# A down projection by seven products: additions to the residual given a later place in the schedule, and one weight difference formed later

## Chip, cores and metric

The kernel runs on one core of one Trainium2 chip. The metric is the device time of one execution in microseconds, lower being better. The kernel before took 1417.21 us (the median of three runs, 1415.67 to 1417.69). Data lies in HBM; SyncE issues the transfers (DMAs) of weights into SBUF, TensorE multiplies into banks of PSUM, VectorE and ScalarE work on SBUF and PSUM. Each engine takes its instructions in the order in which they were put into its queue.

## The reference, cut to what matters

The program is a decoder trunk of two layers over 512 tokens and 1024 features: a gated DeltaNet mixer with a gated MLP behind it, then sliding-window attention with a gated MLP. The change lies in the last product of the MLPs, the down projection (`@ w_down` below), whose result is added to the residual stream `h`.

```python
SEQ = 512; D_MODEL = 1024; D_FF = 2816
def rmsnorm(x, w):
    xf = x.astype(jnp.float32)
    y = xf * lax.rsqrt(jnp.mean(xf * xf, axis=-1, keepdims=True) + EPS)
    return (y * w.astype(jnp.float32)).astype(x.dtype)
...
# every layer: a mixer, then
#   u, g = up projection of rmsnorm(h); a causal convolution of width 3; act(.) * (.)
#   h = h + (that) @ w_down          # 512 x 2816 times 2816 x 1024
# and, behind the last layer, a final rmsnorm
```

## The kernel before, in words

**Layout.** Features lie on the 128 partitions and tokens along the free axis: `h[m]`, for m = 0 to 7, is a tile of 128 features by 512 tokens (the first pair shows in the trace as `h`, pairs behind it as `h` or `pz`). The 2816 inner features of the MLP are 22 tiles of 128.

**A product in three.** Each f32 operand is split into a high part (`whi`, `xh`: a cast by ScalarE, L132, L155, L172) and the rest (`wlo`, `xl`: a subtraction by VectorE, L133, L156, L173). Each product of two tiles is three matmuls: high by high, high by low, low by high. In the up and other projections these are L162 to L164, 512 tokens wide; in the down projection L1052 to L1054, 256 wide.

**The MLP.** `ffn` takes the inner features in two halves, of 12 tiles (six pairs) and of 10 (five pairs). For each half it computes the up projections and forms from them the operands of the seven products (`forms`: VectorE at L1001 to L1007). Then it runs the down projection of this half for the eight output tiles, as four pairs `m2`. So there are four such stretches in the program, two in each layer. The last pair of the last one is computed directly (`last_mm`, L957 to L970) and goes straight into the final norm (`final`, from L1102).

**Seven products (L1039 to L1099).** A block product of two by two blocks (two of inner features and two of output features for the weights, and two halves of the tokens for the inputs) takes seven products of blocks in place of eight. Their inputs are sums and differences of blocks. Weights are combined in place by VectorE: A21 += A22 (L1063), A11 = A21 - A11 (L1071), A12 -= A11 (L1072) and A22 -= A11 (L1080), in a `stage` tile which holds three (or two) pairs of inner tiles; `u` = 0 and 1 are the two `stage` tiles of one pair of output tiles. `cast` splits half 0 of such a tile (blocks A11 and A21) or half 1 (A12 and A22) when it is called; `cast_to(w4, ...)` splits A22 for the seventh product (L155, L156). The products add up in four banks of PSUM: `a` in a bank of tag d (3 buffers), `b` in g (2), `d` in s (2), and `c` in p (1), or in d for odd pairs; the seventh, `e`, is in g, or in p for odd pairs.

**Additions.** `add` (L1056 and L1057) adds a bank to quarters of the residual, on VectorE. With u = 1 four of them follow their products at once: bank a to h11, b to h11, d to h22, c to h21, each 128x256. At the end come bank a once more to three quarters (L1094, 128x768), bank d to h12 (L1095) and bank e to two quarters (L1098, 128x512). A bank is free for the next pair when its last addition has read it.

**What sets the order.** The code is written as generators whose steps are called in a fixed turn: the pairs m2 = 0 and 1 of a stretch in the turn 0, 1, 0, 0, 1, 1, then three steps of 2 and three of 3. From this program order a scheduler builds, before the program is compiled, the order of each engine's queue. An instruction has a priority from its place in the program; `tc.high_priority(n)` moves those inside it ahead, and a negative n puts them back. Buffers (`stage` has 2 and a third, `st`; `whi` and `wlo` have 3 each) are assigned at the same time. The next weights are loaded by SyncE (L1034) into a `stage` buffer once its last reader is done.

Of the kernel before, what the change touches and what calls it, by code (L numbers as in the profile page):

```python
# [12 lines left out]
ALU = mybir.AluOpType  # L13
# [4 lines left out]
P = 128  # L18
# [23 lines left out]
def kernel(  # L42
# [27 lines left out]
    V, S, G, PE, SP = nc.vector, nc.scalar, nc.gpsimd, nc.tensor, nc.sync  # L70
# [42 lines left out]
    def bank(tag):  # L113
        return psum.tile([P, T], F32, tag=tag, bufs=BANKS[tag], name=nm(tag))
# [13 lines left out]
    def cast(st, kt, half, m=P):  # L128
        hi = wpool.tile([P, 8, P], F32R, tag="whi", bufs=3, name=nm("whi"))
        lo = wpool.tile([P, 8, P], F32R, tag="wlo", bufs=3, name=nm("wlo"))  # L130
        src = st[:, :kt, half * P : half * P + m]
        S.copy(hi[:, :kt, :m], src)  # L132
        V.tensor_tensor(lo[:, :kt, :m], src, hi[:, :kt, :m].bitcast(F32), op=ALU.subtract)  # L133
        return hi, lo
# [14 lines left out]
    def weights():  # L149
        return [wpool.tile([P, 8, P], F32R, tag=t, bufs=3, name=nm(t)) for t in ("whi", "wlo")]  # L150

    def cast_to(w, at, src):
        n = src.shape[1]
        hi, lo = [t[:, at : at + n, :] for t in w]
        S.copy(hi, src)  # L155
        V.tensor_tensor(lo, src, hi.bitcast(F32), op=ALU.subtract)  # L156
# [106 lines left out]
    for k in range(KD):  # L263
        ps = bank("g") if k % 2 else bank("s")
# [502 lines left out]
    for i, line in enumerate(ORDER):  # L767
        for word in line.split():
            a, n = word[0], [int(d) for d in word[1:]]
# [41 lines left out]
    def wide(role):  # L811
        return pair(nxt("wide", YROLE), F32R)
# [6 lines left out]
    for h2 in range(HV // 2):  # L819
        a, b = wide("G"), wide("L")  # L820
# [26 lines left out]
    for m2 in range(KD // 2):  # L847
        sts = [load_stage(a_w_out[0], 1024 * u, 8, 256 * m2) for u in range(2)]
        for j in range(2):
            m = 2 * m2 + j  # L850
            ps = bank("d")
# [184 lines left out]

    def seven_products(sts, srcs, parts, sevens, hp, odd):  # L1039
        h11, h12, h21, h22 = [hp[:, i, HALF[u]] for i in range(2) for u in range(2)]  # L1040
        n = len(sevens)

        def blocks(u):
            e, o = slice(0, 2 * len(parts[u]), 2), slice(1, 2 * len(parts[u]), 2)
            return sts[u][:, e, 0:P], sts[u][:, o, 0:P], sts[u][:, e, P : 2 * P], sts[u][:, o, P : 2 * P]

        def product(ps, w, at, form, u, first=True, step=2):
            for i, k in enumerate(parts[u]):
                hi, lo = sevens[k][form]
                wk = at + step * i  # L1050
                kw = dict(skip_group_check=not first)
                PE.matmul(ps, w[0][:, wk, :], hi, start=first and k == 0, stop=False, **kw)  # L1052
                PE.matmul(ps, w[0][:, wk, :], lo, start=False, stop=False, **kw)  # L1053
                PE.matmul(ps, w[1][:, wk, :], hi, start=False, stop=k == n - 1, **kw)  # L1054

        def add(dst, ps):  # L1056
            V.tensor_tensor(dst, dst, ps, op=ALU.add)  # L1057

        a, b, d, c = [bank(t)[:, 0:256] for t in ("d", "g", "s", "d" if odd else "p")]
        for u in range(2):  # L1060
            A11, A12, A21, A22 = blocks(u)
            nk, end = len(parts[u]), u == 1
            V.tensor_tensor(A21, A21, A22, op=ALU.add)  # L1063
            w = cast(sts[u], 2 * nk, 0)
            product(a, w, 0, "B11", u)
            if end:
                add(h11, a)
            product(b, w, 1, "B21", u)
            if end:
                add(h11, b)  # L1070
            V.tensor_tensor(A11, A21, A11, op=ALU.subtract)  # L1071
            V.tensor_tensor(A12, A12, A11, op=ALU.subtract)  # L1072
            w = cast(sts[u], 2 * nk, 1)
            product(d, w, 0, "T1", u)
            if end:
                add(h22, d)
            product(c, w, 1, "T4", u)
            if end:
                add(h21, c)
            V.tensor_tensor(A22, A22, A11, op=ALU.subtract)  # L1080
            yield
        e = bank("p" if odd else "g")[:, 0:256]
        w4 = weights()
        for u in range(2):
            w = cast(sts[u], 2 * len(parts[u]), 0)
            product(a, w, 0, "T2", u, first=False)
            product(d, w, 1, "B22", u, first=False)
            cast_to(w4, 4 * u, blocks(u)[3])

        add(hp.rearrange("p u (v t) -> p (u v) t", v=2)[:, 1:4, :], a.unsqueeze(1).to_broadcast([P, 3, 256]))  # L1090
        add(h12, d)
        for u in range(2):
            product(e, w4, 4 * u, "T3", u, step=1)
        add(hp[:, 1, :].rearrange("p (u t) -> p u t", u=2), e.unsqueeze(1).to_broadcast([P, 2, 256]))  # L1094
        yield  # L1095


# [346 lines left out]
```

## Time and profile before

| what | value |
|---|---|
| three runs | 1417.21, 1415.67, 1417.69 us; median 1417.21 |
| profiled execution | span 1412.6 us; its own time is not printed beside it, the median lies 4.6 us above the span |
| traffic | 151.80 MB, 107 GB/s in the mean; queue q1 takes 33.2% of 16 DMA engines |
| L162, L163, L164 on TensorE | 1128 of each, 444.2, 444.0 and 441.9 us busy (overlapping) |
| L132 casts of `stage` on ScalarE | 234, 227.4 us, mean 976 ns |
| L133 corrections of `stage` on VectorE | 234, 263.4 us, mean 1128 ns |
| L133 corrections of `st` on VectorE | 30, 26.8 us, mean 899 ns |
| loads `stage` from w_down on SyncE's queue | 16 of 768 KB, 4.3 us from issue to landing |
| loads `st` from w_down | 8 of 768 KB, 5.3 us |

How to read it: the span is the time from the first to the last instruction of one profiled execution. An engine's busy share is a mean over stages with different limits, so what a change of one stage is worth is read from the waits in that stage. PE is the matmuls of TensorE, PEld its loads of the stationary operand, DVE is VectorE, ACT ScalarE, SP SyncE. A row of the timeline gives start, duration, engine, line, operation and tiles, and in brackets the idle time before it and what ended that.

### The profile page before, as it was taken

The page shows a single profiled execution, that of the slowest core. Times are in us where ns is not written, and L with a number is a line of the kernel's source. Part 1 is how long each engine was busy: PE and PEld are TensorE (multiplying, and loading weights), DVE is VectorE, ACT ScalarE, POOL GpSimd, SP SyncE. Part 2 cuts the span into 40 slices and gives each one's busy share as a digit, 9 for nine tenths or more (in the row PEclk, how much of TensorE's full clock was granted, in tenths as well). Part 3 has the DMA queues.
Part 4 walks back from the last instruction along what each step waited for, and adds up shares of the span by engine and source line. Part 5 has one row for each costly group of instructions (what it writes and reads, how often), then busy time and mean ns, then how long its engine had stood idle before and what let it go on. Part 6 is the DMA issues. An engine that isn't in the chain of part 4 may idle for free.

```text
span 1412.6 us, 21751 instructions
## 1 busy us (share of the span) xinstructions
PE 1384.7 (98%) x8370; PEld 1167.1 (83%) x8370; DVE 1108.1 (78%) x2070; ACT 748.1 (53%) x1470; POOL 15.6 (1%) x37
## 2 busy tenths in 40 slices
PE   7999999999999999999999999999999999999998
PEld 5787888878877888888988889777788888988897
DVE  4996896978856438879878889788668888878996
ACT  7764566656658225444344446567544444444543
POOL 1000000000100000000000000000000000000000
PEclk9999999999999999999999999999999999999999
DMA  5333254172465323221443223322132231432222
GB/s 161 92 103 115 79 175 126 61 231 84 140 225 159 119 90 112 90 90 46 135 150 119 75 79 109 109 71 76 61 112 90 90 101 49 146 106 82 92 75 75
DMA packets 162299, 151.80 MB, mean 107 GB/s; under 512 B 24148, under 2 KB 150677, under 8 KB 162197
## 3 DMA queue, kind: packets, MB, share of 16 engines
q1 hardware_dynamic: 159938, 150.22, 33.2%
q8 instruction: 66, 1.08, 0.3%
q10 hardware_dynamic: 2259, 0.20, 0.1%
q14 instruction: 36, 0.29, 0.1%
HBM read 133.60 MB, written 15.75 MB: 106 GB/s over the span
## 4 chain that ended last, share of the span: by engine, by line
PE 87%; DVE 6%; DMA 2%; ACT 2%; issue 1%; SPq 0%; DVEq 0%; ACTq 0%
PE d L162 20%; PE d L163 20%; PE d L164 20%; PE g L198 2%; DVE wlo L133 2%; PE d L1054 1%; PE d L1207 1%; PE d L1211 1%; PE d L1209 1%; PE d L1052 1%; PE d L1053 1%; PE s L1054 1%; PE s L1052 1%; PE s L1053 1%; PE s L659 1%
## 5 line engine op out<-in xcount | busy, mean ns | idle before, releaser
L162 PE MATMUL d<-xh,whi 128*128 128x512 f32 x1128 | 444.2, 394 | 0.2
L163 PE MATMUL d<-xl,whi 128*128 128x512 f32 x1128 | 444.0, 394 | 0.0
L164 PE MATMUL d<-xh,wlo 128*128 128x512 f32 x1128 | 441.9, 393 | 0.3 <-DVE wlo L156 0.3
L132 ACT CAST whi<-stage 128x1024 fp32r<-128x1024 f32 (+2 forms) x234 | 227.4, 976 | 247.7 <-PE d L163 165.1
L133 DVE TENSOR_TENSOR wlo<-stage,whi 128x1024 fp32r<-128x1024 f32 (+2 forms) x234 | 263.4, 1128 | 70.4 <-ACT whi L132 69.6
L162 PEld LDWEIGHTS d<-xh,whi 128*128 128x128 f32 x1128 | 211.7, 188 | 44.9 <-ACT xh L172 0.5
L164 PEld LDWEIGHTS d<-xh,wlo 128*128 128x128 f32 x1128 | 211.6, 188 | 44.6 <-DVE wlo L156 0.7
L163 PEld LDWEIGHTS d<-xl,whi 128*128 128x128 f32 x1128 | 211.7, 188 | 43.2 <-issue 0.5
L280 DVE SCALAR_TENSOR_TENSOR acc<-d,cwc,acc 128x511 f32<-128x511 f32 (+2 forms) x96 | 70.7, 739 | 8.7 <-ACT acc L277 7.9
L913 DVE TENSOR_TENSOR sz<-d,p6s 128x512 f32<-128x512 f32 x59 | 40.6, 688 | 42.9 <-PE d L164 40.7
L935 ACT ACTIVATE dt<-dt 128x512 f32<-128x512 f32 x44 | 27.8, 631 | 78.3 <-DVE dt L918 78.3
L918 DVE SCALAR_TENSOR_TENSOR dt<-sz,fcw,dt 128x511 f32<-128x511 f32 (+1 forms) x60 | 44.8, 747 | 1.8 <-ACT dt L916 0.9
L918 DVE SCALAR_TENSOR_TENSOR va<-sz,fcw,va 128x511 f32<-128x511 f32 (+1 forms) x58 | 43.3, 747 | 0.9
L561 DVE TENSOR_TENSOR sT<-sT,p6s 64x31 f32<-64x31 f32 (+15 forms) x124 | 40.9, 330 | 2.0
L555 DVE TENSOR_TENSOR p6s<-sN,sT 64x31 f32<-64x31 f32 (+15 forms) x124 | 40.7, 328 | 1.9
L1276 ACT ACTIVATE dt<-dt,sm 128x256 f32<-128x256 f32 (+1 forms) x64 | 30.1, 471 | 21.5 <-DVE sm L1259 21.5
L132 ACT CAST whi<-st 128x768 fp32r<-128x768 f32 (+1 forms) x30 | 23.7, 792 | 30.5 <-PE g L1053 9.0
L913 DVE TENSOR_TENSOR zl<-d,p6s 128x512 f32<-128x512 f32 x29 | 20.0, 688 | 17.8 <-PE d L164 17.8
L682 ACT ACTIVATE rq<-o 128x128 f32<-128x128 f32 x64 | 19.0, 301 | 25.4 <-DVE o L677 22.3
L937 DVE TENSOR_TENSOR va<-dt,va 128x512 f32<-128x512 f32 x44 | 30.4, 690 | 1.2
L133 DVE TENSOR_TENSOR wlo<-st,whi 128x768 fp32r<-128x768 f32 (+1 forms) x30 | 26.8, 899 | 2.2 <-ACT whi L132 2.2
L916 ACT ACTIVATE dt<-sz,normc,fcw 128x512 f32<-128x512 f32 x30 | 24.5, 815 | 6.5 <-DVE sz L913 6.0
(770 smaller groups left out, 2876.2 us busy)
## 6 DMA issues: line engine op xcount, KB each, us to landing
stage<-in_ffn_w_up_dram SPq DMA_DIRECT2D x44, 1024.0 KB, 4.8
stage<-in_a_w_in_dram SPq DMA_DIRECT2D x23, 1024.0 KB, 5.8
stage<-in_ffn_w_down_dram SPq DMA_DIRECT2D x16, 768.0 KB, 4.3
stage<-in_a_w_out_dram SPq DMA_DIRECT2D x8, 1024.0 KB, 5.0
st<-in_ffn_w_down_dram SPq DMA_DIRECT2D x8, 768.0 KB, 5.3
zd<-sz SPq DMA_DIRECT2D x16, 256.0 KB, 2.6
od<-o SPq DMA_DIRECT2D x16, 256.0 KB
stage<-in_b_w_q_dram SPq DMA_DIRECT2D x4, 1024.0 KB, 5.0
```

The source lines that it names most:

```text
L132: S.copy(hi[:, :kt, :m], src)
L133: V.tensor_tensor(lo[:, :kt, :m], src, hi[:, :kt, :m].bitcast(F32), op=ALU.subtract)
L162: PE.matmul(ps, hi[:, k, :m], xh[k], start=first and k == 0, stop=False)
L163: PE.matmul(ps, hi[:, k, :m], xl[k][:], start=False, stop=False)
L164: done.append(PE.matmul(ps, lo[:, k, :m], xh[k], start=False, stop=last and k == kt - 1))
L280: V.scalar_tensor_tensor(acc[:, d:], ps[:, : T - d], col, acc[:, d:], op0=ALU.mult, op1=ALU.add)
L555: V.tensor_tensor(tv, N[:, s, s + 1 : 32].unsqueeze(2).to_broadcast([64, n, m]), Tm[:, s : s + 1, 0:m].to_broadcast([64, n, m]), op=ALU.mult,)
L561: V.tensor_tensor(Tm[:, s + 1 : 32, 0:m], Tm[:, s + 1 : 32, 0:m], tv, op=ALU.subtract)
L913: V.tensor_tensor(u[:], ps[:], rs[:], op=ALU.mult)
L918: V.scalar_tensor_tensor(acc[:, d:], u[:, : T - d], tap(2 - d, t), acc[:, d:], op0=ALU.mult, op1=ALU.add)
L937: V.tensor_tensor(b[:], a[:], b[:], op=ALU.mult)
L1276: S.activation(ej, ej, AF.Exp, bias=ngm[:, i : i + 1], scale=-1.0, accum_out=den[:, i : i + 1])
```

## The change

All of it lies in `seven_products`. First, each addition to the residual is issued inside `tc.high_priority(-later)`, with `later` = 60 for the four that follow the products of u = 1, and END = 100 for the three at the end. Second, A22 -= A11 of both `u` is formed in the last step of the generator, just ahead of the `cast_to` that reads it, in place of the step of products T1 and T4.

```diff
+    END = 100
+
     def seven_products(sts, srcs, parts, sevens, hp, odd):
...
-        def add(dst, ps):
-            V.tensor_tensor(dst, dst, ps, op=ALU.add)
+        def add(dst, ps, later=60):
+            with tc.high_priority(-later):
+                V.tensor_tensor(dst, dst, ps, op=ALU.add)
...
             if end:
                 add(h21, c)
-            V.tensor_tensor(A22, A22, A11, op=ALU.subtract)
             yield
...
             product(a, w, 0, "T2", u, first=False)
             product(d, w, 1, "B22", u, first=False)
-            cast_to(w4, 4 * u, blocks(u)[3])
-
-        add(hp.rearrange("p u (v t) -> p (u v) t", v=2)[:, 1:4, :], a.unsqueeze(1).to_broadcast([P, 3, 256]))
-        add(h12, d)
+            A11, A12, A21, A22 = blocks(u)
+            V.tensor_tensor(A22, A22, A11, op=ALU.subtract)
+            cast_to(w4, 4 * u, A22)
+
+        add(hp.rearrange("p u (v t) -> p (u v) t", v=2)[:, 1:4, :], a.unsqueeze(1).to_broadcast([P, 3, 256]), END)
+        add(h12, d, END)
...
-        add(hp[:, 1, :].rearrange("p (u t) -> p u t", u=2), e.unsqueeze(1).to_broadcast([P, 2, 256]))
+        add(hp[:, 1, :].rearrange("p (u t) -> p u t", u=2), e.unsqueeze(1).to_broadcast([P, 2, 256]), END)
```

The numbers of instructions on every engine stay as they were (1967 rows on VectorE, 6929 on TensorE and 1030 on ScalarE), and SyncE's and GpSimd's queues keep their order. In the changed file the matmuls are L1054 to L1056, the addition is L1060, and the subtractions are L1066, L1074, L1075 and L1091. The scheduler gives other orders on VectorE, TensorE and ScalarE at three kinds of places.

**VectorE, first stretch of the first layer**, where pairs m2 = 0 and 1 overlap (`st_995`, `stage_6181` and `stage_6179` are weight tiles, `h_4550` is the residual; d, g, s and p are banks). Before:

```order
L1080 TENSOR_TENSOR st_995_6183<-st_995_6183 128x3x128
L133 TENSOR_TENSOR wlo_6293<-stage_6181,whi_6292 128x768
L133 TENSOR_TENSOR wlo_6319<-stage_6181,whi_6318 128x768
L1071 TENSOR_TENSOR stage_6181<-stage_6181 128x3x128
L1057 TENSOR_TENSOR h_4550<-h_4550,d_6187 128x256
L1072 TENSOR_TENSOR stage_6181<-stage_6181 128x3x128
L1057 TENSOR_TENSOR h_4550<-h_4550,g_6188 128x256
L1080 TENSOR_TENSOR stage_6181<-stage_6181 128x3x128
L1057 TENSOR_TENSOR h_4550<-h_4550,s_6189 128x256
L133 TENSOR_TENSOR wlo_6347<-stage_6179,whi_6346 128x768
L1057 TENSOR_TENSOR h_4550<-h_4550,p_6190 128x256
L156 TENSOR_TENSOR wlo_6345<-stage_6179,whi_6344 128x384
```

At the same place in the changed kernel:

```order
L133 TENSOR_TENSOR wlo_6291<-stage_6181,whi_6290 128x768
L133 TENSOR_TENSOR wlo_6317<-stage_6181,whi_6316 128x768
L1074 TENSOR_TENSOR stage_6181<-stage_6181 128x3x128
L133 TENSOR_TENSOR wlo_6344<-stage_6179,whi_6343 128x768
L1075 TENSOR_TENSOR stage_6181<-stage_6181 128x3x128
L156 TENSOR_TENSOR wlo_6342<-stage_6179,whi_6341 128x384
L1060 TENSOR_TENSOR h_4550<-h_4550,d_6187 128x256
L1091 TENSOR_TENSOR stage_6181<-stage_6181 128x3x128
L1060 TENSOR_TENSOR h_4550<-h_4550,g_6188 128x256
L1060 TENSOR_TENSOR h_4550<-h_4550,s_6189 128x256
```

The subtraction on `st` now stands behind these rows, and the correction and the split of `stage_6179` (L133 and L156) stand ahead of the four additions and not among and behind them.

**VectorE, end of the first layer** (behind the last products of the second stretch; `xl` are the low parts of the next norm's input, `f` and `gr` weights of the shared K/V projection, L866 sums squares). Before:

```order
L173 SCALAR_TENSOR_TENSOR xl_8389<-h_4550,normc_102,xh_8388 128x512
L1057 TENSOR_TENSOR pz_4552<-pz_4552,d_8209 128x768
L173 SCALAR_TENSOR_TENSOR xl_8393<-pz_4551,normc_102,xh_8392 128x512
L1057 TENSOR_TENSOR pz_4552<-pz_4552,s_8211 128x256
L173 SCALAR_TENSOR_TENSOR xl_8397<-pz_4551,normc_102,xh_8396 128x512
L1057 TENSOR_TENSOR pz_4552<-pz_4552,p_8301 128x512
L156 TENSOR_TENSOR wlo_8410<-f_8364,whi_8409 128x256
L173 SCALAR_TENSOR_TENSOR xl_8401<-pz_4552,normc_102,xh_8400 128x512
```

In the changed kernel:

```order
L173 SCALAR_TENSOR_TENSOR xl_8397<-pz_4551,normc_102,xh_8396 128x512
L156 TENSOR_TENSOR wlo_8410<-f_8364,whi_8409 128x256
L156 TENSOR_TENSOR wlo_8410<-f_8365,whi_8409 128x256
L156 TENSOR_TENSOR wlo_8410<-f_8366,whi_8409 128x256
L156 TENSOR_TENSOR wlo_8410<-gr_8367,whi_8409 128x256
L156 TENSOR_TENSOR wlo_8445<-f_8364,whi_8444 128x256
L156 TENSOR_TENSOR wlo_8445<-f_8365,whi_8444 128x256
L156 TENSOR_TENSOR wlo_8445<-f_8366,whi_8444 128x256
L156 TENSOR_TENSOR wlo_8445<-gr_8367,whi_8444 128x256
L1060 TENSOR_TENSOR pz_4552<-pz_4552,d_8209 128x768
```

The last three additions now stand behind all eight splits of the next projection's weights.

**TensorE and VectorE, second stretch of the first layer, the one bank of tag p** (`p_7981` is the seventh product of pair 1, `p_8053` the fourth product of pair 2 in the same bank). TensorE before, where the products' matmuls are mixed:

```order
L1053 MATMUL g_8051<-qT_7384,whi_8055 128x256
L1054 MATMUL g_8051<-qT_7384,wlo_8056 128x256
L1052 MATMUL s_8052<-qT_7056,whi_8079 128x256
L1053 MATMUL s_8052<-nt_7059,whi_8079 128x256
L1052 MATMUL p_8053<-nt_7059,whi_8079 128x256
L1053 MATMUL p_8053<-nt_7062,whi_8079 128x256
L1054 MATMUL s_8052<-qT_7056,wlo_8080 128x256
L1052 MATMUL s_8052<-sy_7224,whi_8079 128x256
```

VectorE in the changed kernel, around the addition that frees this bank:

```order
L1060 TENSOR_TENSOR h_4550<-h_4550,s_7789 128x256
L1074 TENSOR_TENSOR stage_8048<-stage_8048 128x2x128
L133 TENSOR_TENSOR wlo_8123<-stage_8048,whi_8122 128x512
L1075 TENSOR_TENSOR stage_8048<-stage_8048 128x2x128
L1091 TENSOR_TENSOR stage_8046<-stage_8046 128x3x128
L1060 TENSOR_TENSOR h_4550<-h_4550,p_7981 128x512
```

TensorE in the changed kernel starts that bank behind the products s of both `u`, and the matmuls stand in the program's order, product by product, three to a pair of tiles:

```order
L1056 MATMUL g_8051<-vt_7715,wlo_8103 128x256
L1054 MATMUL s_8052<-ktok_7555,whi_8122 128x256
L1055 MATMUL s_8052<-ktok_7555,whi_8122 128x256
L1056 MATMUL s_8052<-ktok_7555,wlo_8123 128x256
L1054 MATMUL p_8053<-nt_7059,whi_8079 128x256
L1055 MATMUL p_8053<-nt_7062,whi_8079 128x256
L1056 MATMUL p_8053<-nt_7059,wlo_8080 128x256
```

## The prediction on record

> **What bounds the kernel now.** I read the page's first part, then the busy time by stretch, then the waits of TensorE's queue, then the timeline.
>
> ```profile
> span 1412.6 us, 21751 instructions
> PE 1384.7 (98%) x8370; PEld 1167.1 (83%) x8370; DVE 1108.1 (78%) x2070; ACT 748.1 (53%) x1470; POOL 15.6 (1%) x37
> ```
>
> TensorE is busy for 98% of the span. The number of its matmuls does not change, so this change can only win back time in which TensorE waits, and only in the four stretches of `seven_products` and just behind them. How much is that? The windows are the four down projections (first, second, fourth and fifth row) and, in the third row, the time behind the second, to the next norm.
>
> ```profile
> core 0: us, PE busy (x) PEld busy (x) DVE busy (x) ACT busy (x) POOL busy (x), PEclk, DMA share, GB/s
> 655.72:718.75 63.03, 61.89 (x506) 60.79 (x504) 55.71 (x96) 25.79 (x36) 0.00 (x0) 1.00 0.35 114
> 827.58:881.89 54.31, 52.17 (x421) 50.81 (x420) 51.51 (x100) 30.00 (x52) 0.00 (x0) 1.00 0.31 94
> 881.89:895.67 13.78, 13.29 (x61) 10.13 (x60) 12.51 (x22) 7.71 (x11) 0.00 (x0) 1.00 0.34 115
> 1174.35:1237.14 62.79, 61.84 (x505) 60.80 (x504) 56.02 (x95) 26.83 (x37) 0.00 (x0) 1.00 0.34 110
> 1345.97:1386.53 40.56, 39.34 (x318) 38.32 (x317) 38.54 (x76) 19.93 (x32) 0.00 (x0) 1.00 0.24 79
> ```
>
> A busy PE is not yet PE at its pace, so I take the pace from neighbours in the timeline that wait for nothing: a 256-wide matmul starts 0.12 us behind the one before, a 512-wide one 0.23 us.
>
> ```profile
> 836.33 0.28 PE L1053 MATMUL d<-at,whi 128*128 128x256 f32 x1
> 836.45 0.28 PE L1052 MATMUL g<-at,whi 128*128 128x256 f32 x1
> 883.65 0.39 PE L164 MATMUL d<-xh,wlo 128*128 128x512 f32 x1
> 883.88 0.39 PE L162 MATMUL d<-xh,whi 128*128 128x512 f32 x1
> ```
>
> 504 matmuls at 0.12 us are 60.48 us, so the first stretch (63.03) holds 2.55 us of waits and the third (62.79) 2.31. 420 are 50.40, so the second (54.31) holds 3.91. 315 are 37.80, which with two or three short transposes leaves about 2.5 us in the fourth (40.56). Behind the second stretch the gaps between the starts of 512-wide matmuls above their pace add up to about 1.65 us (the largest of them is quoted below). **The cap on the gain is thus 2.55 + 3.91 + 1.65 + 2.31 + 2.5 = 12.9 us.** The granted clock is 1.00 in all five windows, so the throttle takes nothing there.
>
> What are the waits for? By line, over the whole run:
>
> ```profile
> PEld d L1054 <- DVE wlo L133: 4.8, 9, 1.2
> PEld s L1054 <- DVE wlo L133: 2.4, 5, 0.6
> PEld d L1052 <- ACT whi L132: 1.7, 3, 0.8
> PEld p L1052 <- ACT whi L155: 0.6, 3, 0.2
> ```
>
> TensorE waits in these stretches above all for VectorE's corrections `wlo` (4.8 + 2.4 us), and no row names a bank that an addition has not freed. The order of VectorE before, shown with the change, says why: additions, which nobody needs soon, stand on VectorE ahead of corrections, which TensorE needs at once.
>
> **The change part by part.** It removes and adds no instruction. What counts is what stands behind what. First the price of a place on VectorE, start to next start.
>
> ```profile
> 664.39 0.55 DVE L1080 TENSOR_TENSOR st<-st 128x384 f32<-128x384 f32 x1
> 664.86 1.81 DVE L133 TENSOR_TENSOR wlo<-stage,whi 128x768 fp32r<-128x768 f32 x2
> 665.86 0.39 PE L1054 MATMUL d<-at,wlo 128*128 128x256 f32 x1 [0.39 <-DVE wlo L133]
> 667.93 0.42 DVE L1057 TENSOR_TENSOR h<-h,g 128x256 f32<-128x256 f32 x1
> 669.07 0.95 DVE L133 TENSOR_TENSOR wlo<-stage,whi 128x768 fp32r<-128x768 f32 x1
> 670.27 0.55 DVE L156 TENSOR_TENSOR wlo<-stage,whi 128x384 fp32r<-128x384 f32 x1
> ```
>
> A subtraction of 128x384 takes 664.86 - 664.39 = 0.47 us of the queue; a correction of 128x768 takes 1.81 - 0.95 = 0.86 (two in 1.81, the last 0.95).
>
> [...]
>
> *First stretch, the wait at 665.86.* There TensorE waits 0.39 us for the correction that starts at 664.86, behind the A22 subtraction at 664.39. In the changed order that subtraction stands behind; the correction starts 0.47 us sooner, so the wait goes, but for about 0.1 us of neighbours' unevenness. Gain 0.4.
>
> *First stretch, the weights that come late.* The next weights go into the `stage` buffer whose last reader is the split at 670.27 (a row of the chain of waits, then the timeline):
>
> ```profile
> 670.85 4.59 DMA stage<-in_ffn_w_down_dram
> ```
>
> ```profile
> 675.54 1.57 ACT L132 CAST whi<-stage 128x768 fp32r<-128x768 f32 x2 [5.25 <-DMA stage<-in_ffn_w_down_dram]
> 676.43 0.39 PE L1052 MATMUL d<-at,whi 128*128 128x256 f32 x1 [0.35 <-ACT whi L132]
> 680.74 0.39 PE L1054 MATMUL s<-ktok,wlo 128*128 128x256 f32 x1 [0.40 <-DVE wlo L133]
> ```
>
> The transfer starts at 670.85, just when that split has ended, lands 4.59 us later, ScalarE's cast starts at 675.54 after 5.25 us of idleness, and TensorE waits at 676.43 and again, for the corrections behind, at 680.74. The starts between 676.4 and 681 lie 1.8 us above their pace in all. Before, three additions, two subtractions and two corrections stand between 667.06 and that split; in the changed order the corrections and this split go first: 664.39 + 2 x 0.86 + 0.47 (L1074) + 0.86 + 0.47 (L1075) + 0.47 = 668.4 us for its end; the cast that it needs may make it 668.8. The transfer starts about 2.1 us sooner, the weights are there at 673.3, and the cast (0.84 us) ends by 674.2, where TensorE needs it at about 675.3. So all 1.8 us go. What is late next is small: the corrections behind additions in the last third, 0.35 us in all. Gain of the stretch 0.4 + 1.8 = **2.2**.
>
> *Third stretch.* The same code, with 2.31 us of waits. The same two places hold about 2.0 of them: **2.0**.
>
> *Second and fourth stretch, additions ahead of corrections.* With pairs of 768 and 512 wide tiles there is less time for each correction.
>
> ```profile
> 839.65 0.42 DVE L1057 TENSOR_TENSOR h<-h,p 128x256 f32<-128x256 f32 x1
> 839.99 0.42 DVE L1080 TENSOR_TENSOR stage<-stage 128x256 f32<-128x256 f32 x1
> 840.33 0.95 DVE L133 TENSOR_TENSOR wlo<-st,whi 128x768 fp32r<-128x768 f32 x1
> 841.33 0.39 PE L1054 MATMUL d<-qT,wlo 128*128 128x256 f32 x1 [1.00 <-DVE wlo L133]
> 846.17 0.62 ACT L132 CAST whi<-st 128x512 fp32r<-128x512 f32 x1 [5.32 <-PE g L1053]
> 846.84 0.39 PE L1052 MATMUL d<-at,whi 128*128 128x256 f32 x1 [0.56 <-ACT whi L132]
> ```
>
> Four additions end with the one at 839.65; each has 0.34 us of the queue (839.99 - 839.65). The L1080 subtraction follows, and only then the correction at 840.33, for which TensorE waits 1.00 us at 841.33. In the changed order the four additions and this subtraction stand behind the correction. They took 5 x 0.34 = 1.7 us of places of which not all was in its way; I leave 0.15 of the wait, as the cast ahead of it is not sooner. Here too a transfer starts sooner, by about 2.6 us by the same count, so the wait for the cast that starts at 846.17 (0.56 us at 846.84, 0.73 with its neighbours) goes. The fourth stretch has the same first place:
>
> ```profile
> 1359.64 0.39 PE L1054 MATMUL d<-vt,wlo 128*128 128x256 f32 x1 [1.00 <-DVE wlo L133]
> ```
>
> *The bank of tag p, a new wait.* The deferred additions hold their banks longer, and p has one buffer.
>
> ```profile
> 689.29 0.68 DVE L1057 TENSOR_TENSOR h<-h,p 128x512 f32<-128x512 f32 x1
> 691.75 0.28 PE L1052 MATMUL p<-nt,whi 128*128 128x256 f32 x1
> 856.54 0.68 DVE L1057 TENSOR_TENSOR h<-h,p 128x512 f32<-128x512 f32 x1
> 858.47 0.28 PE L1052 MATMUL p<-nt,whi 128*128 128x256 f32 x1
> ```
>
> Before, the bank's last addition starts at 689.29 and TensorE writes it again at 691.75; in the second stretch these are 856.54 and 858.47. In the changed order of the first stretch I count VectorE's queue up to that addition: it ends at about 688.3, and TensorE, without its waits, is there at 689.5: 1.1 us of slack. In the second, additions, two subtractions of L1074 and L1075, a correction and one of L1091 stand ahead; it ends at 858.7, and TensorE comes at 858.3: a **new wait of about 0.45 us**. Queued behind that matmul are all of TensorE's next products, so the 0.45 counts in full, and the cast for a `whi` buffer that these products release comes later by as much (another 0.65). With some unevenness about 1.7 of the second stretch's 3.91 us stay: gain **2.2**. In the fourth, of 2.5 us about 1.0 stay: gain **1.5**.
>
> *Behind the second stretch.*
>
> ```profile
> 882.43 0.68 DVE L1057 TENSOR_TENSOR pz<-pz,p 128x512 f32<-128x512 f32 x1
> 885.48 0.50 PE L164 MATMUL d<-xh,wlo 128*128 128x512 f32 x1 [0.30 <-DVE wlo L156]
> 894.76 1.05 PE L869 MATMUL g<-ones,ol 128*128 128x1 f32 x8
> ```
>
> The last addition at 882.43 goes behind eight splits; TensorE's wait at 885.48 for such a split goes, and with it most of 1.65 us. The norm that needs these additions has its matmuls at 894.76; three additions at 0.95 us or less behind 6 us of splits end before 890, so they are covered by 4 us; without this cover each would cost its whole 0.95. Some low parts `xl` come just in time (within 0.1 us by my count), so 0.6 us stay: gain **1.05**. The end of the second layer, where the last additions go behind the direct pair's work, I cost at nothing: its cover is TensorE's matmuls of that pair. For the bounds I take one operation of 0.68 us (the row at 882.43) uncovered or covered: 0.7 either way.
>
> The sum is 2.2 + 2.0 + 2.2 + 1.05 + 1.5 = **8.95 us**. The profiled execution has a span of 1412.6 us, to which 1403.65 would answer; the median of the runs lies 4.6 us above the span, and with these 4.6 the time is 1408.3 us.
>
> **The rivals.**
>
> *VectorE is the bound of the short stretches.* It is busy for 51.51 of 54.31 us and 38.54 of 40.56; moving an addition back then only moves the wait to a later matmul. For: these shares. Against: busy durations overlap (1.81 for two of 0.95), so its places take some 43 of 54 us. Then only the long stretches gain, 4.2 us: 1413.0.
>
> *The change does not bring what it says.* A correction needs its cast `whi` first, of which there are three buffers; ScalarE's casts often wait for TensorE to release one. If these casts end last wherever a correction was late, another wait takes the place of the one removed. For: the `whi` waits of 1.7 and 0.6 us. Against: 7.2 us are put down to `wlo`. It leaves perhaps 1 us: 1416.
>
> *Slower: the deferred additions hold bank p.* Its one buffer is taken again twice or so in each stretch. TensorE waits once VectorE comes to the additions more than 1.1 us later than walked (long stretches); in the short ones this is so already. For: 60 to 100 places of priority are a wide berth, and VectorE has little idle time. Against: additions are still in VectorE's queue where the order shows them, a few rows behind. At 4 us late each, two waits of 4 - 1.1 = 2.9 us in long and two of 4 + 0.45 = 4.45 in short stretches cost 14.7 us, less 8.95: 5.8 us slower, 1423.
>
> **How the numbers follow.** The walk has a chance of 0.62, the VectorE bound 0.20, no effect 0.11, the bank 0.07. The likeliest is the walk: 1408.3 us. A measurement of this kernel can tell about 0.2% (2.8 us) from no change, so faster means below 1414.4. The walk and the first rival lie there, but a weak form of either would not: 0.80. Same is 0.13, slower 0.07. The range goes from all waits gone and 0.7 us at the end of the second layer (1417.2 - 12.9 - 0.7 = 1403.6) up to the first rival with 1.5 us to spare: 1414.5; it leaves out the two other rivals, 0.18.
>
> **What would show it.** In the changed profile the first and third stretch should take about 60.8 us, the second about 52.1, the fourth about 39.1. TensorE's waits for L133 at the line of the low part should fall from 7.2 to below 2 us; the transfer of 670.85 should start near 668.7. A new wait of a p matmul for an addition should appear once, near 0.45 us, in the second stretch. I am wrong if the stretches keep their lengths and the waits only change their names (`whi` for `wlo`), if p's matmuls wait for additions by 1 us or more in every stretch, or if the time behind 881.89 grows.

## The result and the profile after

The changed kernel takes **1409.21 us** (median of six runs, 1407.28 to 1412.14); the kernel before took 1416.51 us in the runs beside it. The ratio is **0.9945, with a 95% interval from 0.9932 to 0.9957**: 7.8 us faster by the ratio (the two medians differ by 7.3). One of the six runs of the kernel before took 6826.91 us; it lies far outside the others and the ratio leaves it out. The forecast was 1408.3 us. The first lines of the page of the changed kernel:

```profile
span 1407.5 us, 21786 instructions
PE 1382.0 (98%) x8370; PEld 1168.1 (83%) x8370; DVE 1107.1 (79%) x2070; ACT 747.5 (53%) x1470; POOL 14.6 (1%) x37
```

The two profiled spans differ by 5.1 us only. This is no contradiction: the part ahead of the first down projection, in which both kernels have the same code, took 655.72 us in the profile of before and 658.31 in that of the changed kernel (their first windows begin there). In ten more profiles below it takes 655 to 661 us. One part of the difference can be seen: from 45.49 to 48.91 us the granted clock was 0.50 in the changed kernel's profile and 1.00 in that of before. So spans of single profiles can't be compared to a few us here; the stretches can, to 0.2 us. The busy time by stretch, with the same columns as before:

```profile
core 0: us, PE busy (x) PEld busy (x) DVE busy (x) ACT busy (x) POOL busy (x), PEclk, DMA share, GB/s
658.31:719.13 60.82, 60.79 (x505) 60.57 (x504) 55.38 (x96) 25.97 (x36) 0.00 (x0) 1.00 0.37 118
827.96:879.88 51.92, 50.94 (x421) 50.56 (x420) 50.92 (x100) 29.98 (x52) 0.00 (x0) 1.00 0.35 109
1171.42:1233.14 61.72, 61.43 (x506) 60.74 (x504) 55.89 (x95) 26.84 (x37) 0.00 (x0) 1.00 0.35 111
1341.97:1381.13 39.16, 38.40 (x317) 37.98 (x316) 38.04 (x75) 19.80 (x32) 0.00 (x0) 1.00 0.25 81
```

From the end of the second stretch to the start of the third it is 0.92 us less. First the row of before, from its profile:

```profile
881.89:1174.35 292.46, 290.99 (x1615) 235.31 (x1613) 227.67 (x495) 162.05 (x336) 0.00 (x0) 1.00 0.27 87
```

The same part in the changed kernel:

```profile
879.88:1171.42 291.54, 290.30 (x1614) 235.61 (x1613) 227.43 (x496) 162.05 (x336) 0.00 (x0) 1.00 0.27 86
```

| part | before | after | gain | forecast of the gain |
|---|---|---|---|---|
| first stretch | 63.03 | 60.82 | 2.21 | 2.2 |
| second | 54.31 | 51.92 | 2.39 | 2.2 |
| behind the second | 292.46 | 291.54 | 0.92 | 1.05 |
| third | 62.79 | 61.72 | 1.07 | 2.0 |
| fourth | 40.56 | 39.16 | 1.40 | 1.5 |
| behind the fourth | 26.12 | 26.35 | -0.23 | 0 |
| sum | | | 7.76 | 8.95 |

Behind the first and behind the third stretch nothing changed (108.83 us each). The sum of the parts, 7.76 us, agrees with the runs (7.8 by the ratio). The waits of TensorE's loads in these lines, over the whole run, show what is left:

```profile
PEld d L1054 <- ACT whi L155: 1.2, 1, 1.2
PEld d L1056 <- DVE wlo L133: 0.9, 3, 0.5
PEld d L1054 <- ACT whi L132: 0.9, 1, 0.9
```

The waits for corrections fell from 4.8 + 2.4 to 0.9 us. Two new ones of about 1 us have come; they are read below, and they are not for the engine that these rows name.

**The first stretch, as walked.** The timeline of the changed kernel, where the next weights are loaded:

```profile
671.10 3.28 SPq L1034 DMA_DIRECT2D stage<-in_ffn_w_down_dram  x2
675.45 0.84 ACT L132 CAST whi<-stage 128x768 fp32r<-128x768 f32 x1 [2.52 <-DMA stage<-in_ffn_w_down_dram]
```

This stretch begins 2.59 us later in this profile, so the transfer starts, on the clock of before, at 668.5 (forecast 668.7; before 670.85), and the cast at 672.9 (forecast 673.3; before 675.54). All gaps from 676 to 681 us are gone; 0.35 us of waits are left in the stretch.

**The third stretch, which fell short.** The same place, from the timeline and, for the second row, from the chain of waits:

```profile
1184.20 0.37 SPq L1034 DMA_DIRECT2D stage<-in_ffn_w_down_dram  x1
1189.97 2.30 ACT L132 CAST whi<-stage 128x768 fp32r<-128x768 f32 x3 [3.93 <-DMA stage<-in_ffn_w_down_dram]
1191.85 0.38 PE L1056 MATMUL d<-qT,wlo 128*128 128x256 f32 x1 [0.25 <-DVE wlo L133]
```

```profile
1184.20 5.67 DMA stage<-in_ffn_w_down_dram
```

The transfer starts 12.8 us into the stretch, just as in the first (671.10 - 658.31), but takes 5.67 us where that of the first stretch has landed within 4.35 (675.45 - 671.10). So TensorE still waits here; the last section shows what lies inside this transfer.

**The short stretches, where a wait was exchanged.** The timeline of the changed kernel in the second stretch, at the place where before the correction came late:

```profile
838.50 0.95 DVE L133 TENSOR_TENSOR wlo<-st,whi 128x768 fp32r<-128x768 f32 x1
839.47 0.28 PE L1056 MATMUL p<-S,wlo 128*128 128x256 f32 x1
839.84 0.42 DVE L1091 TENSOR_TENSOR stage<-stage 128x256 f32<-128x256 f32 x1
840.17 0.41 DVE L1060 TENSOR_TENSOR h<-h,d 128x256 f32<-128x256 f32 x1
840.73 0.36 PE L1054 MATMUL d<-qT,whi 128*128 128x256 f32 x1 [0.98 <-ACT whi L155]
```

The correction is there at 839.45, in time. But TensorE, done with bank p at 839.47, starts its next product (T2, into bank d) only at 840.73, 1.14 us behind its pace. T2 goes on accumulating in bank a, and the addition of that bank to h11, at 840.17, has to read it first; it ends at 840.58. In the fourth stretch it is the same, and there the row names the addition:

```profile
1353.84 0.41 DVE L1060 TENSOR_TENSOR h<-h,d 128x256 f32<-128x256 f32 x1
1354.40 0.36 PE L1054 MATMUL d<-vt,whi 128*128 128x256 f32 x1 [0.76 <-DVE h L1060]
```

Both matmuls start 0.15 us behind the end of that addition. The row of the second stretch names a cast that ended at about the same time (840.69); which is right was left to the experiments.

**Bank p and the time behind the second stretch.** The addition that frees bank p, and TensorE's next write to it:

```profile
858.84 0.68 DVE L1060 TENSOR_TENSOR h<-h,p 128x512 f32<-128x512 f32 x1
859.66 0.35 PE L1054 MATMUL p<-nt,whi 128*128 128x256 f32 x1
```

The wait was expected at 0.45 us and more behind it; the gaps here come to 0.22. Behind the second stretch the deferred additions end well ahead of the norm's matmuls:

```profile
882.21 0.94 DVE L1060 TENSOR_TENSOR pz<-pz,d 128x768 f32<-128x768 f32 x1
884.61 0.68 DVE L1060 TENSOR_TENSOR pz<-pz,p 128x512 f32<-128x512 f32 x1
892.38 0.95 PE L869 MATMUL g<-ones,ol 128*128 128x1 f32 x8
```

### The profile page after: what moved, and what is told of

It reads as the page before. It is cut to its first block, busy times and chain, and to the rows that moved or that the text cites. A ratio compares the mean times of both kernels' runs of the same rounds, so it can differ in the third digit from the quotient of the medians.

```text
span 1407.5 us, 21786 instructions
## 1 busy us (share of the span) xinstructions
PE 1382.0 (98%) x8370; PEld 1168.1 (83%) x8370; DVE 1107.1 (79%) x2070; ACT 747.5 (53%) x1470; POOL 14.6 (1%) x37
## 4 chain that ended last, share of the span: by engine, by line
PE 90%; DVE 3%; DMA 3%; ACT 3%; issue 1%; ACTq 0%; DVEq 0%; SPq 0%
PE d L162 20%; PE d L163 20%; PE d L164 20%; PE g L198 2%; PE d L1056 2%; PE d L1054 2%; PE d L1055 1%; PE d L1211 1%; PE d L1215 1%; PE d L1213 1%; PE s L1054 1%; PE s L1056 1%; PE s L1055 1%; DMA ol<-od 1%; PE s L659 1%; PE p L1307 1%
## 5 line engine op out<-in xcount | busy, mean ns | idle before, releaser
L133 DVE TENSOR_TENSOR wlo<-stage,whi 128x1024 fp32r<-128x1024 f32 (+2 forms) x234 | 263.7, 1129 | 71.1 <-ACT whi L132 69.7
L133 DVE TENSOR_TENSOR wlo<-st,whi 128x768 fp32r<-128x768 f32 (+1 forms) x30 | 26.9, 900 | 1.8 <-ACT whi L132 1.4
```

## The experiments

Two questions were open. Which part of the change does what: the additions, the subtraction, the four or the last three? And what sets the new wait at 11.4 us into the short stretches: the bank that an addition holds, or a cast for want of a `whi` buffer? All kernels below are edits of the changed kernel. The stretches, from each kernel's one profile, in us, with the ratio to the kernel before. Gains in us below are (1 - ratio) times 1416.5 us; in the runs beside these experiments the kernel before took 1417.5 to 1417.8 us.

| kernel | first | behind it | second | behind it | third | fourth | ratio (95%) |
|---|---|---|---|---|---|---|---|
| before | 63.03 | 108.83 | 54.31 | 292.46 | 62.79 | 40.56 | |
| changed | 60.82 | 108.83 | 51.92 | 291.54 | 61.72 | 39.16 | 0.9945 (0.9932 to 0.9957) |
| e1 additions only | 61.76 | 108.84 | 53.04 | 291.51 | 62.95 | 41.95 | 0.9990 (0.9978 to 1.0002) |
| e2 subtraction only | 61.94 | 109.76 | 53.05 | 292.15 | 62.09 | 39.80 | 0.9982 (0.9973 to 0.9992) |
| e3 four deferred | 60.82 | 108.98 | 51.77 | 295.00 | 61.66 | 38.89 | 0.9964 (0.9951 to 0.9976) |
| e4 last three deferred | 61.43 | 109.73 | 52.56 | 291.29 | 61.05 | 40.08 | 0.9958 (0.9946 to 0.9970) |
| e5 two at once | 60.97 | 109.74 | 52.31 | 291.64 | 60.78 | 38.58 | 0.9949 (0.9930 to 0.9967) |
| e6 own buffer | 60.68 | 108.81 | 52.25 | 291.26 | 61.49 | 39.31 | 0.9954 (0.9938 to 0.9970) |
| e7 both | 60.66 | 108.81 | 52.14 | 291.82 | 60.67 | 38.47 | 0.9939 (0.9922 to 0.9956) |
| e8 further | 61.88 | 108.83 | 56.77 | 290.93 | 62.61 | 42.84 | 1.0012 (0.9997 to 1.0026) |
| e9 changed again | 60.83 | 108.85 | 51.93 | 291.52 | 61.57 | 39.18 | 0.9936 (0.9919 to 0.9952) |
| e10 both again | 60.68 | 108.81 | 52.13 | 291.82 | 60.67 | 38.61 | 0.9932 (0.9918 to 0.9947) |

**e1, the additions alone.** The subtraction is back in the step of T1 and T4:

```diff
                 add(h21, c)
+            V.tensor_tensor(A22, A22, A11, op=ALU.subtract)
             yield
...
-            A11, A12, A21, A22 = blocks(u)
-            V.tensor_tensor(A22, A22, A11, op=ALU.subtract)
-            cast_to(w4, 4 * u, A22)
+            cast_to(w4, 4 * u, blocks(u)[3])
```

> All seven additions are deferred as in the changed kernel, the subtraction A22 -= A11 is back in its old place. Theory (each of the two parts takes work out of the way of a correction or of a split that frees a weight buffer): the first wait of the long stretches (0.5 us each) is back, the weights still come about 1.5 us sooner than before, the time behind the second stretch stays 0.9 us shorter. Gain 6.3 us, about 1410.2 where the kernel before takes 1416.5. Rival A (the additions alone do it): the whole gain, 7.3 to 7.8 us. Rival B (the subtraction alone does it): at most 2 us.

Measured: 1416.14 us, 1.4 us less than before and within the uncertainty of no change. The expected 6.3 us did not come, and neither did Rival A. The first wait of the long stretches is back (0.54 us, with the gap behind it 0.64, where the changed kernel has 0.29), as expected, but a new one stands in all four, for the addition of bank a. The timeline of this kernel in the fourth stretch:

```profile
1355.14 0.41 DVE L1060 TENSOR_TENSOR h<-h,d 128x256 f32<-128x256 f32 x1
1355.70 0.36 PE L1054 MATMUL d<-vt,whi 128*128 128x256 f32 x1 [1.79 <-DVE h L1060]
```

Here TensorE waits 1.95 us, in the second stretch 2.00, in the long ones 0.58 each. With the subtractions in their old place, more stands ahead of the deferred addition; again the matmul starts 0.15 us behind its end. In the fourth stretch a second loss follows, read in the last section.

**e2, the subtraction alone.** `add` loses its `tc.high_priority`:

```diff
-            with tc.high_priority(-later):
-                V.tensor_tensor(dst, dst, ps, op=ALU.add)
+            V.tensor_tensor(dst, dst, ps, op=ALU.add)
```

> Only the subtraction A22 -= A11 is moved, the additions keep their old priority. Theory: the first wait of the long stretches goes (0.4 us each), the split that frees the weight buffer ends about 1.1 us sooner in place of 2.3, so some 0.7 us of the late weights stay in each long stretch; nothing behind the second stretch. Gain 3 us, about 1413.5. Rival A: under 1 us. Rival B: 7 us or more. The two parts overlap where both advance the same split, so the gains of this run and of the one with the additions alone add up to more than the whole.

Measured: 1414.81 us, 2.6 us less, about as expected; the long stretches keep 1.2 and 1.3 us of waits about the late weights (0.7 expected). But the last sentence is wrong: 1.4 and 2.6 us add up to 4.0, little over half of the 7.8 us of both together. The table shows where. In the first two stretches the parts nearly add up: 1.27 (e1) and 1.09 (e2) against 2.21, then 1.27 and 1.26 against 2.39. What is missing lies in three other places. In the fourth stretch e1 is 1.39 us longer than before, by its wait for bank a and the lower clock behind it. In the third e1 gains nothing, as its weights come late there (0.95 us of waits, with a slow transfer as in the changed kernel). And e2 loses 0.93 us behind the first stretch (109.76), where the next up projection's weights, issued at the same place, land 1.0 us later than in the changed kernel.

**e3, the four deferred, and e4, the last three.** `END = 0` in the one, `later=0` as the default in the other, with the priority left alone for 0:

```diff
-            with tc.high_priority(-later):
+            if later:
+                with tc.high_priority(-later):
+                    V.tensor_tensor(dst, dst, ps, op=ALU.add)
+            else:
                 V.tensor_tensor(dst, dst, ps, op=ALU.add)
```

> The changed kernel, but the last three additions of each pair keep their old priority (only the four that follow the products of u = 1 are deferred). Theory: the stretches stay within 0.4 us each of the changed kernel's 60.8, 51.9, 61.7 and 39.2 us, the 0.9 us behind the second stretch is lost. Gain 6.7 us, about 1409.8. If instead it is the last three that hold corrections up, over 3 us of the gain is lost.

> The changed kernel, but the four additions that follow the products of u = 1 keep their old priority (only the last three are deferred). Theory: the stretches as with the moved subtraction alone, plus the 0.9 us behind the second stretch: gain 4 us, about 1412.5. The wait of TensorE at 11.4 us into the short stretches (1.14 and 0.92 us in the changed kernel), which ends 0.15 us behind the addition of bank d to h, changes: if that addition sets it, it falls by the 0.35 us by which that addition ends behind the cast.

Measured: 1412.46 us for e3, 5.1 us less than before where 6.7 were expected. The stretches are as expected, but the time behind the second is 3.46 us longer than in the changed kernel and not 0.9. The last three additions stand ahead of a split there:

```profile
884.26 0.79 PE L164 MATMUL d<-xh,wlo 128*128 128x512 f32 x1 [1.67 <-DVE wlo L156]
```

A wait of 1.85 us against the pace, and about 1.6 us more by a lower clock that begins at the end of this wait. For e4, 1411.59 us, 6.0 us less where 4 were expected: the wait at 11.4 us fell from 1.14 to nothing in the second stretch (0.28 us stay 0.7 us later, for a correction), not by 0.35, and from 0.92 to nothing in the fourth (0.10 us stay behind it). That speaks for the addition as its whole cause.

**e5, the additions of banks a and d at once.** These two are the ones whose bank is accumulated into again by the same pair:

```diff
-                add(h11, a)
+                add(h11, a, 0)
...
-                add(h22, d)
+                add(h22, d, 0)
```

> The changed kernel, but the additions of the banks that the same pair goes on accumulating into (bank a to h11, bank d to h22) keep their old priority; the other five stay deferred. Bank theory (TensorE cannot go on accumulating into bank a before its addition to h11 has read it, so a deferred addition is itself waited for): in the short stretches the wait at 11.4 us (1.14 and 0.92 us in the changed kernel) falls by the 0.25 to 0.35 us by which that addition ended behind the cast, and no wait is put down to an addition; the long stretches lose at most 0.5 us each, since corrections again stand behind two additions. Total about that of the changed kernel, gain 7.3 us. Buffer theory (the cast for want of a whi buffer sets that wait): the wait keeps its 1.14 us.

Measured: ratio 0.9949. The wait is gone altogether, not by 0.35 us. The timeline of this kernel in the second stretch, TensorE alone:

```profile
836.94 0.28 PE L1056 MATMUL p<-S,wlo 128*128 128x256 f32 x1
837.06 0.28 PE L1054 MATMUL d<-qT,whi 128*128 128x256 f32 x1
```

T2 follows bank p at the pace of 0.12 us. The buffer theory fails here: nothing was done for the cast. The cast that was taken for the limit is that of u = 1; T2 begins with u = 0, whose cast had long ended (at 837.57 us in the changed kernel). The fourth stretch is 0.58 us shorter than in the changed kernel, the second 0.39 longer: other waits appear 31 to 33 us into it, the largest of them (0.52 us) for a correction. And 0.91 us are lost behind the first stretch, as in e2 and e4, where the next weights land late. These three leave the additions of banks a and d early, but so do e7 and e10, which lose nothing there (108.81 us), so the place of the additions alone is not the reason.

**e6, a buffer of its own for the seventh product's high parts.**

```diff
-        w4 = weights()
+        w4 = [wpool.tile([P, 6, P], F32R, tag="w4hi", bufs=1, name=nm("w4hi")), wpool.tile([P, 8, P], F32R, tag="wlo", bufs=3, name=nm("wlo"))]
...
-            cast_to(w4, 4 * u, A22)
+            cast_to(w4, 3 * u, A22)
...
-            product(e, w4, 4 * u, "T3", u, step=1)
+            product(e, w4, 3 * u, "T3", u, step=1)
```

> The changed kernel, but the high parts of the seventh product's weights have a buffer of their own, so that three whi buffers are left for the casts. In this order the addition of bank a to h11 stands about 0.6 us later on VectorE in the second stretch. Bank theory: the wait at 11.4 us there rises from 1.14 to about 1.6 us, though the cast comes sooner. Buffer theory: it falls below 0.4 us, and the second and fourth stretch are 0.7 us shorter each.

Measured: ratio 0.9954. The wait grew to 1.77 us in the second stretch (1.6 expected) and 1.52 in the fourth: the bank theory holds, the buffer theory fails with the other sign. The timeline of this kernel:

```profile
843.16 0.41 DVE L1060 TENSOR_TENSOR h<-h,d 128x256 f32<-128x256 f32 x1
843.27 0.41 ACT L155 CAST w4hi<-stage 128x256 fp32r<-128x256 f32 x1 [1.60 <-DVE stage L1091]
843.72 0.36 PE L1054 MATMUL d<-qT,whi 128*128 128x256 f32 x1 [1.61 <-ACT w4hi L155]
```

The row puts the wait down to a cast into `w4hi`, which this matmul does not read; its start is again 0.15 us behind the addition. This is the wrong releaser that made the buffer look likely.

**e7, both edits.** e5 and e6 together.

> Both edits: own buffer for the seventh product's high parts, and the additions of banks a and d at their old priority. Both theories: the wait at 11.4 us in the short stretches falls below 0.4 us, since neither the cast nor the addition is late; second and fourth stretch 51.2 and 38.5 us, the long ones at most 0.5 us longer than in the changed kernel. Gain 8.5 us, the fastest kernel so far. If a correction takes over as the one that ends last (the VectorE bound), the short stretches stay at 51.9 and 39.2.

Measured: ratio 0.9939. The wait is gone in both short stretches, the long ones are 60.66 and 60.67 us, the fourth 38.47 as expected. The second kept 52.14 (51.2 expected): at 17 and at 31 to 33 us into it other waits of 1.6 us in all are left, small ones that the rows mostly do not name; they were not followed further.

**e8, deferred further.** `later=200` and `END = 300`.

> The changed kernel with the additions deferred further: 200 in place of 60 and 300 in place of 100. Bank theory: waits of TensorE for additions of bank d grow in all four stretches, by 0.3 us in the long ones (one more subtraction ahead of the addition) and 0.7 us or more in the short ones; gain 5 us, about 2.8 us less than the changed kernel's. If nobody needs the additions soon, the gain stays at 7.3 to 7.8 us or grows.

Measured: ratio 1.0012, the whole gain lost where a gain of 5 us was expected. The waits for bank a are 0.92 us in the long stretches and 2.54 and 2.33 us in the short ones:

```profile
843.22 0.42 DVE L1060 TENSOR_TENSOR h<-h,d 128x256 f32<-128x256 f32 x1
843.78 0.36 PE L1054 MATMUL d<-qT,whi 128*128 128x256 f32 x1 [2.38 <-DVE h L1060]
```

Behind each of the two long waits the clock was lower for 3.4 us, which the expectation did not count. Nor did it count the waits late in the stretches: 1.33 us in the second and 0.72 in the fourth for a correction, and 0.71 us in the third for the addition out of bank p, which ends 0.15 us ahead of the matmul that waits.

**e9 and e10, once more side by side.**

> The changed kernel once more, on the same chip and beside the same runs of the kernel before as the next one. Time: ratio 0.9945 as measured (0.9932 to 0.9957). In its profile the four stretches take 60.8, 51.9, 61.7 and 39.2 us again, and the third stretch again waits about 0.4 us at 20.4 us into it, because the transfer that starts 12.8 us into it takes about 5.7 us there; if that was chance, it takes about 4.4 us as in the first stretch, and the third stretch is 60.8 us long. The part ahead of the first stretch, whose code is the same in all kernels, lies anywhere between 654.7 and 660.8 us.

> Own buffer for the seventh product's high parts and the additions of banks a and d at their old priority, once more, beside the changed kernel. By the traces its four stretches and what lies behind them are 1.4 us shorter than the changed kernel's, so a ratio of about 0.9935 to the kernel before, 0.1% ahead of the changed kernel. If the difference was only in the one profile, both have the same ratio.

Measured: 1409.03 us with a ratio of 0.9936, and 1408.09 with 0.9932. The stretches are the same to 0.15 us. The transfer in the third stretch took long again (5.52 us, from 12.8 us into the stretch), so this was not the chance of one execution. In the traces e10 is 1.2 us ahead of the changed kernel; the timed runs can't tell the two apart.

## Why the prediction was right, point by point

- **The cap and where it lies.** The gains came in the four stretches and just behind the second, out of TensorE's waits, as laid down; the granted clock stayed at 1.00 in them.
- **Corrections ahead of additions in the long stretches.** Right in its size (2.21 against 2.2) and in its two places: the first wait fell with the subtraction from 0.64 to 0.29 us (in e1, which has it in the old place, it is 0.64 again; in e2 0.29), and the transfer came 2.3 us sooner.
- **The third stretch** was mis-sized by 0.9 us: "The same two places hold about 2.0 of them" took the transfer of the first stretch for its own. It took 5.67 and 5.52 us in two profiles of the changed kernel. It is not the time of its issue that decides: in e7 and e10 it is issued 0.7 us later, its cast starts 4.4 us after the issue, and the third stretch is 60.67 us long; in e1 it is issued 0.9 us later, and the cast starts 5.8 us after the issue. The last section shows what sets the slow transfers apart.
- **The step that failed** is the sentence that additions are work "which nobody needs soon", and with it the term "I leave 0.15 of the wait" in the short stretches. The additions of banks a and d are needed soon: the same pair goes on accumulating into these banks. The wait for a correction (1.16 us against the pace in each of the two) was exchanged for one for the addition of bank a (1.14 and 0.92), which e4 and e5 take away and e1, e6 and e8 lengthen. That the total of these stretches held all the same is luck: the walk had counted other waits too high, by about as much. Of 0.45 + 0.65 us behind bank p only 0.22 came, and the small waits late in the second stretch went as well. TensorE's own order changed too where bank p is taken again; no run here separates the share of that.
- **Behind the second stretch** 0.92 us against 1.05, with the additions covered as walked. e3 shows the price of the old place in this order: 3.5 us, of which about 1.6 are the lower clock.
- **The rivals.** VectorE as the bound of the short stretches: no, they gained 2.39 and 1.40 us with VectorE as busy as before (50.92 of 51.92 us and 38.04 of 39.16). No effect: no. The slower rival had the right mechanism, but the bank that costs most is not p, which two pairs share; it is bank a, which one pair uses twice. Bank p cost 0.14 us in the changed kernel (the matmul at 859.66) and at most 0.71 us in e8. The addition of bank a is waited for as soon as it ends behind the last matmul of the fourth product, which in the short stretches it does already in the changed kernel; e8 shows its price.

## What to carry to other kernels

Before work is put back in a queue, look for its readers and for the buffer that it reads: an addition out of an accumulator frees it, and the next writer may be the same product a few matmuls on (in e8 TensorE waited 2.54 us for such an addition). Defer the additions whose bank is next written late, and look twice at those whose bank is written again soon. Leaving these early took their wait away (e5, e7), though the timed runs show no further gain: 0.9949 and 0.9939 lie within the uncertainty of the changed kernel's 0.9945. Try such a pair of edits together, since here each alone brought 1.4 and 2.6 us and both 7.8. A releaser named by the profile is to be checked against the data that the instruction reads; a constant distance to the end of another instruction (about 0.15 us in the changed kernel, e1, e6 and e8) points to the true one.

## What the runs showed of the hardware

**The clock.** Some waits of TensorE of about 2 us cost more than themselves here (in e1, e3 and e8): the granted clock was 0.50 for 3.4 us from about their end. From e8, the time just behind the 2.54 us wait, and the slow time:

```profile
843.80:845.00 1.20, 1.20 (x10) 1.20 (x11) 0.91 (x4) 0.00 (x0) 0.00 (x0) 1.00 0.81 219
845.00:848.40 3.40, 3.40 (x18) 3.40 (x18) 1.14 (x3) 0.62 (x1) 0.00 (x0) 0.50 0.68 222
```

There are 18 matmuls in 3.4 us at clock 0.50, where the pace of 0.12 us would allow 28. From e3, behind its wait of 1.85 us:

```profile
884.26:887.40 3.14, 3.14 (x7) 2.47 (x8) 3.14 (x9) 0.21 (x1) 0.00 (x0) 0.50 0.00 0
```

The same followed the waits of 1.95 us (e1, fourth stretch) and 2.33 us (e8, fourth); it did not follow one of 2.00 us (e1, second) or of 1.77 (e6). The clock fell 1.2 to 1.3 us after the end of the wait in e1 and e8, and 0.1 us before it in e3. The starts of the slow times lie on a grid in time. The one from 45.49 us in the profile of the changed kernel is 3.413 us long, and where a profile has several, their starts lie whole multiples of this apart (45.49 and 1404.00 us in the changed kernel are 398 of them, 44.47 and 884.15 in e3 are 246, 845.01 and 1363.84 in e8 are 152). These are windows of that grid in e1, two about the wait in the second stretch and two from the wait in the fourth:

```profile
834.78:838.20 3.42, 2.77 (x22) 2.37 (x20) 3.42 (x8) 1.47 (x3) 0.00 (x0) 1.00 0.01 2
838.20:841.61 3.41, 2.10 (x17) 2.13 (x18) 2.50 (x7) 0.42 (x2) 0.00 (x0) 1.00 0.57 165
1353.61:1357.02 3.41, 1.62 (x14) 1.45 (x13) 3.13 (x8) 0.92 (x2) 0.00 (x0) 1.00 0.44 124
1357.02:1360.43 3.41, 3.41 (x18) 3.41 (x18) 1.29 (x3) 0.62 (x1) 0.00 (x0) 0.50 0.84 257
```

The wait of 2.00 us is cut by an edge at 838.20, so that its two windows hold 1.1 and 1.4 us of waits (counted against the pace, with smaller ones). The wait of 1.95 us lies in one window, which holds 2.0 us, and the next window is slow. In the four stretches and 15 us behind each, over all twelve profiles, each of the four windows with 2.0 to 2.3 us of waits was followed by a slow one, and no window with 1.84 us or less was. So in these profiles the slow time went with the waits within one window of the grid (2.0 us and more of its 3.41), and not with the length of a wait by itself (2.00 us in e1, cut by an edge, brought none).

**The slow transfers.** The profile lists packets of 16 KB of a queue q8, of the kind "instruction": 66 in before and 66 in the changed kernel, each of which takes 0.9 to 2.1 us. In the changed kernel one lies inside the transfer in the third stretch (1184.20 to 1189.87). In e7 none lies between the issue in that stretch (1184.64) and 1189.0, when the cast has started:

```profile
q1 hardware_dynamic: 1192, 1.20, 67.3%
q8 instruction: 1, 0.02, 1.1%
```

```profile
q1 hardware_dynamic: 816, 0.82, 62.5%
```

In the third stretch of the changed kernel, e1, e3, e6 and e9 such a packet starts 2.9 to 3.7 us after the issue, and the cast starts 5.6 to 5.8 us after the issue. In before, e2, e4, e5, e7 and e10 it starts ahead of the issue, and the cast 4.4 to 4.5 us after the issue. (In e8 the cast waits for TensorE, so the landing can't be read.) The weights that come late behind the first stretch fit as well: in e2, e4 and e5 the packet starts 3.3 to 3.4 us after their issue, and their cast 6.1 to 6.3 us after it; in the other nine 4.1 to 4.4 us, and the cast 5.0 to 5.3. This is a coincidence in all 23 transfers; no run moved such a packet alone, so the cause is not shown.
